# First norm's statistics from a second, row-wise copy of the input, loaded in four parts, with the inverse roots broadcast through a line in HBM

## The chip, the cores and the metric

The kernel runs on one core of a Trainium2 chip. The metric is the device time of one execution in microseconds. The times of the kernel before are the median, the lowest and the highest of three runs; one execution more was taken by the hardware profiler, and all rows of the profile come from that one.

## The reference, cut to what matters

A trunk of two layers on one sequence of 256 tokens with 2048 features, all in float32. The change touches only the first norm and the first projection; what follows in the same layer shows who reads their results.

```python
def rmsnorm(x, g):
    x32 = x.astype(jnp.float32)
    y = x32 * lax.rsqrt(jnp.mean(jnp.square(x32), axis=-1, keepdims=True) + NORM_EPS)
    return (y * g.astype(jnp.float32)).astype(x.dtype)

def short_conv_mixer(u, w_in, conv_w, w_out):
    proj = u @ w_in                                  # 2048 -> 3 * 2048
    xin, gate_c, gate_b = jnp.split(proj, 3, axis=-1)
    v = gate_c * xin
    S = v.shape[1]
    vp = jnp.pad(v, ((0, 0), (CONV_WIDTH - 1, 0), (0, 0)))
    conv = sum(conv_w[k] * vp[:, k:k + S] for k in range(CONV_WIDTH))
    return (gate_b * conv) @ w_out

# layer 0
u = rmsnorm(h, mix_pre_g[0])
m = short_conv_mixer(u, a_w_in[0], a_conv_w[0], a_w_out[0])
h = h + rmsnorm(m, mix_post_g[0])
...                                                  # squared-ReLU MLP, shared K and V,
                                                     # layer 1: stick-breaking attention, MLP
```

## The kernel before

Every float32 product is made of three matmuls of rounded parts: each weight and each input is split into a high part (ACT rounds it, `whi`, L174 or L219) and a low part (DVE subtracts, `wlo`, L185). Weights come in chunks of 128x1024 (512 KB) on SP's queue, five raw buffers deep (`RAW`), and their parts live in a ring of seven (`RING`). `chunk` asks for the splits up to four chunks ahead of the one in use (`AHEAD`).

The order of the instructions on PE is that of the program text. On DVE, ACT and POOL a planner of the framework fixes an order when the program is built, from priorities that follow the text and from its own estimate of when operands are there; on the chip each engine then runs its list strictly in order. A piece of work that the text asks for late can therefore stand early in an engine's list.

The first stage is `convolution`. The input comes transposed (`xT`, features on the partitions, 256 tokens in a row). The norm's gain is multiplied in at once (`enter`), but the norm's factor, one number per token, only after the projection, since it scales whole columns: `r` is the inverse root for each token, on all partitions, and `r2` its square (for the product of two projections).

- In the lead, six tiles of the projection (`lead`) are computed side by side over the 16 input blocks. Meanwhile `squares` makes the squares of the input on ACT (L836) and adds them up on DVE (L838, L840).
- Then come the units of `IN_UNITS`: tiles 0 to 3, then sixteen times a pair and a tile (tiles 4 to 19), then tiles 20 to 25. A tile is 16 high and 16 low matmuls (L813) into one PSUM bank; `IN_BANKS` gives banks 0, 1 and 7 to tiles 0, 1, 2, and bank 6 to tiles 3 to 19. So from tile 4 on, a tile can't start before the bank has been emptied of the one before, by `combined`: ACT copies one half (`half`, L820), DVE adds the other (`sum`, L822). A pair is 21 matmuls of 512 columns (L922 to L924, seven block products in the manner of Strassen and Winograd) that needs sums of input blocks (`sums_of_pair`, L903 to L911) and of weight blocks (`split_seven`, L211). After the eighth pair seven additions on DVE (L933) collect the first result.
- `statistics` runs after tile 0: the two halves of `acc` are added, two passes of a matmul with a matrix of 1/2048 (`ms`, L851) sum over the partitions and spread the result over all of them, and then follow a root on ACT, a reciprocal of 128x256 and a square on DVE.
- `conv_tile` takes three finished tiles (input, gate C, gate B) through product, scaling by `r2`, convolution, scaling by `r` and splitting for the next projection. It is called after tiles 1, 2, 4, 5, 8, 11, 14 and 17; the first and the third of these take the tiles of the lead.
- After tile 21 the text asks for the rows of `x` that the residual needs (`h`, L982, on POOL's queue).

`x4` is a tag with eight buffers of 8 KB per partition: `u` takes four, the last `xsums` two, and `y4` follows.

Of the kernel before, what the change touches and what calls it, by code (L numbers as in the profile page):

```python
# [45 lines left out]
LATER = 7  # L46
# [50 lines left out]
def trunk(ctx, tc, x, xT, vecs, rows, ws, out):  # L97
# [8 lines left out]
    wsplit = ctx.enter_context(tc.tile_pool(name="ws", bufs=RING))  # L106
    psum = ctx.enter_context(tc.tile_pool(name="ps", bufs=1, space=bass.MemoryType.PSUM))
# [663 lines left out]
    def convolution(tmp):  # L771
# [27 lines left out]
        acc = tmp.tile([P, 2 * T], F32, tag="acc", name="acc", bufs=1)  # L799
# [17 lines left out]

        def combined(ps):
            b = tiny("half")
            nc.scalar.activation(b[:], ps[:, T:], AF.Copy)  # L820
            s = tiny("sum", bufs=LEAD + 2)
            nc.vector.tensor_tensor(s[:], ps[:, :T], b[:], op=ALU.add)  # L822
            return s
# [9 lines left out]
        def squares(q, behind):  # L833
            sq = tmp.tile([P, 2 * T], F32, tag="sq", name="sq", bufs=1)
            with tc.issue_after(entered[behind].ins):
                nc.scalar.activation(sq[:], hpair[q], AF.Square)  # L836
            if q == 0:
                nc.vector.tensor_copy(acc[:], sq[:])  # L838
            else:
                nc.vector.tensor_tensor(acc[:], acc[:], sq[:], op=ALU.add)  # L840

# [3 lines left out]
        mean = tmp.tile([P, P], F32, name="mean")  # L845
        nc.vector.memset(mean[:], 1.0 / D)

        def statistics():
            nc.vector.tensor_tensor(acc[:, :T], acc[:, :T], acc[:, T:], op=ALU.add)
            ps = bank(LEAD - 1, "ms")  # L850
            nc.tensor.matmul(ps[:, :T], mean[:], acc[:, :T], start=True, stop=True)  # L851
            r, r2 = tiny("rstd", bufs=1), tiny("rstd2", bufs=1)
            nc.scalar.activation(r[:], ps[:, :T], AF.Sqrt, bias=eps[:])
            nc.vector.reciprocal(r[:], r[:])
            nc.vector.tensor_tensor(r2[:], r[:], r[:], op=ALU.mult)
            scale["r"], scale["r2"] = r, r2

# [94 lines left out]
        for kind, i in IN_UNITS:  # L952
# [10 lines left out]
            if not scale:  # L963
                statistics()
            s = combined(ps)
            if n >= 2 * KD + KD // 2:
                gates[n - 2 * KD] = s
            else:
                new.append(s)
                if lead and len(new) == 2:  # L970
                    conv_tile(LEAD // 3 - len(lead) // 3, *lead[:3])
                    del lead[:3]
                if len(new) == 3:
                    conv_tile(n - 2 * KD, *new)
                    new = []
            if i == KD + 3:
# [571 lines left out]
```

## Time and profile before

| | |
|---|---|
| median of three runs | 2097.27 us (2096.62 to 2098.21) |
| the profiled execution | 2096.79 us, of it 2095.0 us span |
| granted TensorE clock of that execution | 0.998 |
| busy: PE, PE weight load, DVE, ACT, POOL | 99%, 85%, 90%, 70%, 5% of the span |
| lead of the first stage | to about 42 us |
| pairs and tiles of the first stage | about 42 to 260 us |

Times of rows count from the start of the span, in microseconds. A row of the timeline has the start, the duration, the engine, the line, the operation, output and inputs, the shape, how many were merged, and in brackets how long the engine was idle before and what ended that. A row of a group has the busy time and the mean duration in nanoseconds. A row of the waits has the total, the number and the longest. A row of DMA issues has the size of one and the median time from its issue to its landing.

### The profile page before, as it was taken

The page shows a single profiled execution, that of the slowest core. Times are in us where ns is not written, and L with a number is a line of the kernel's source. Part 1 is how long each engine was busy: PE and PEld are TensorE (multiplying, and loading weights), DVE is VectorE, ACT ScalarE, POOL GpSimd, SP SyncE. Part 2 cuts the span into 40 slices and gives each one's busy share as a digit, 9 for nine tenths or more (in the row PEclk, how much of TensorE's full clock was granted, in tenths as well). Part 3 has the DMA queues.
Part 4 walks back from the last instruction along what each step waited for, and adds up shares of the span by engine and source line. Part 5 has one row for each costly group of instructions (what it writes and reads, how often), then busy time and mean ns, then how long its engine had stood idle before and what let it go on. Part 6 is the DMA issues. An engine that isn't in the chain of part 4 may idle for free.

```text
span 2095.0 us, 29733 instructions
## 1 busy us (share of the span) xinstructions
PE 2079.7 (99%) x10566; PEld 1774.8 (85%) x10566; DVE 1888.3 (90%) x2811; ACT 1456.1 (70%) x2132; POOL 112.6 (5%) x137
## 2 busy tenths in 40 slices
PE   9999999999999999999999999999999999999998
PEld 8888888888888888888888888889888888888886
DVE  8999996999999999999766777658999999999997
ACT  8666554776777777777567888547877767677773
POOL 0000000000100101001000000000001010010010
PEclk9999999999999999999999999999999999999999
DMA  8467674677778878779575555665687787787884
GB/s 291 149 204 251 199 248 155 193 231 227 239 221 234 237 217 251 224 230 261 181 220 167 161 161 161 221 181 171 181 256 232 221 241 225 233 245 219 232 241 164
DMA packets 132341, 449.23 MB, mean 214 GB/s; under 512 B 14816, under 2 KB 15072, under 8 KB 131168
## 3 DMA queue, kind: packets, MB, share of 16 engines
q1 hardware_dynamic: 113184, 406.55, 60.9%
q0 software_dynamic: 18720, 40.38, 9.7%
q8 instruction: 83, 1.36, 0.3%
q14 instruction: 66, 0.54, 0.1%
q10 hardware_dynamic: 288, 0.39, 0.1%
HBM read 413.19 MB, written 2.10 MB: 198 GB/s over the span
## 4 chain that ended last, share of the span: by engine, by line
PE 94%; DVE 4%; issue 1%; DMA 1%; ACT 0%; SPq 0%; DVEq 0%; ACTq 0%
PE up L1081 21%; PE up L1088 12%; PE acc L327 7%; PE acc L329 7%; PE acc L328 7%; PE more L1195 5%; PE more L1194 5%; PE more L1196 5%; PE acc L813 5%; PE acc L1194 4%; PE acc L1195 4%; PE acc L1196 4%; DVE wlo L185 1%; PE up L1083 1%; PE tr L264 1%
## 5 line engine op out<-in xcount | busy, mean ns | idle before, releaser
L185 DVE TENSOR_TENSOR wlo<-raw,whi 128x1024 fp32r<-128x1024 f32 (+1 forms) x414 | 495.9, 1207 | 67.6 <-ACT whi L174 67.3
L174 ACT ACTIVATE whi<-raw 128x1024 fp32r<-128x1024 f32 (+1 forms) x414 | 424.7, 1044 | 152.3 <-PE acc L329 63.5
L1081 PE MATMUL up<-u,whi 128*128 128x512 f32 x1952 | 465.0, 389 | 0.0
L1081 PEld LDWEIGHTS up<-u,whi 128*128 128x128 f32 x1952 | 365.0, 188 | 74.7
L1088 PEld LDWEIGHTS up<-u,wlo 128*128 128x128 f32 x2048 | 263.6, 191 | 10.3
L1088 PE MATMUL up<-u,wlo 128*128 128x256 f32 x2048 | 268.1, 283 | 0.0
L211 DVE TENSOR_TENSOR sums<-raw,sums 128x512 f32<-128x512 f32 x260 | 179.3, 690 | 0.9
L187 DVE SCALAR_TENSOR_TENSOR wlo<-raw,gv,whi 128x512 fp32r<-128x512 f32 (+1 forms) x160 | 131.9, 854 | 41.7 <-ACT whi L174 40.9
L174 ACT ACTIVATE whi<-raw,gv 128x512 fp32r<-128x512 f32 (+1 forms) x160 | 121.6, 800 | 48.6 <-PE acc L329 42.2
L327 PE MATMUL acc<-whi,u 128*128 128x512 f32 x384 | 153.1, 399 | 0.1
L329 PE MATMUL acc<-whi,u 128*128 128x512 f32 x384 | 149.9, 390 | 0.0
L328 PE MATMUL acc<-wlo,u 128*128 128x512 f32 x384 | 149.8, 390 | 0.0
L1094 ACT ACTIVATE half<-up 128x256 f32<-128x256 f32 x128 | 49.1, 385 | 129.8 <-PE up L1088 127.2
L1101 POOL DMA_DIRECT2D mg<-more x108 | 94.0, 870 | 825.8 <-ACT more L1156 423.9
L813 PE MATMUL acc<-u,whi 128*128 128x512 f32 x416 | 98.9, 391 | 2.7 <-DVE sum L822 2.7
L211 DVE TENSOR_TENSOR sums<-raw,raw 128x512 f32<-128x512 f32 x130 | 89.8, 691 | 7.2 <-DMA raw<-w_mlp 7.1
L813 PEld LDWEIGHTS acc<-u,whi 128*128 128x128 f32 x416 | 77.4, 188 | 20.5 <-DVE sum L822 3.7
L211 DVE TENSOR_TENSOR sums<-raw 128x512 f32<-128x512 f32 x130 | 89.8, 691 | 2.2 <-DMA raw<-w_mlp 1.6
L329 PEld LDWEIGHTS acc<-whi,u 128*128 128x128 f32 x384 | 72.1, 188 | 15.4
L327 PEld LDWEIGHTS acc<-whi,u 128*128 128x128 f32 x384 | 72.2, 188 | 13.9 <-ACT tk L1380 0.6
L328 PEld LDWEIGHTS acc<-wlo,u 128*128 128x128 f32 x384 | 72.3, 188 | 13.4
L1034 ACT ACTIVATE s<-s 128x256 f32<-128x256 f32 x128 | 52.1, 411 | 12.1 <-DVE s L1033 11.6
(6686 smaller groups left out, 4589.3 us busy)
## 6 DMA issues: line engine op xcount, KB each, us to landing
raw<-w_mlp SPq DMA_DIRECT2D x512, 512.0 KB, 4.6
raw<-w_in SPq DMA_DIRECT2D x94, 512.0 KB, 4.5
mg<-more POOLq DMA_DIRECT2D x108, 256.0 KB, 6.2
raw<-w_out SPq DMA_DIRECT2D x32, 512.0 KB, 4.6
raw<-w_v SPq DMA_DIRECT2D x32, 512.0 KB, 4.5
raw<-w_k SPq DMA_DIRECT2D x32, 512.0 KB, 4.4
raw<-w_q SPq DMA_DIRECT2D x32, 512.0 KB, 4.3
raw<-w_wo SPq DMA_DIRECT2D x32, 512.0 KB, 3.8
```

The source lines that it names most:

```text
L174: rounded = nc.scalar.activation(hi[:, at], raw[i][:, at], AF.Copy, scale=1.0 if gain is None else gain)
L185: nc.vector.tensor_tensor(lo[:, at], t[:, at], hi[:, at].bitcast(F32), op=ALU.subtract)
L211: nc.vector.tensor_tensor(t, x, y, op=ALU.subtract)
L327: nc.tensor.matmul(ps[:], xh, hi[:, a], start=i == 0 and k == 0, stop=False)
L328: nc.tensor.matmul(ps[:], xh, lo[:, a], start=False, stop=False)
L329: nc.tensor.matmul(ps[:], xl, hi[:, a], start=False, stop=i == self.n - 1 and k == self.ks - 1)
L813: nc.tensor.matmul(ps[:, :cols], w, xs[:, :cols], start=k == 0 and part == parts[0], stop=k == KD - 1 and part == parts[1], skip_group_che ...
L1081: nc.tensor.matmul(ps, weight(0, first, m), x, start=k == 0, stop=False)
L1088: nc.tensor.matmul(pss[n][:, :T], weight(1, first, m), x, start=False, stop=k == KD - 1)
L1194: nc.tensor.matmul(self.ps[key][:], xh, hi, start=first, stop=False)
L1195: nc.tensor.matmul(self.ps[key][:], xh, lo, start=False, stop=False)
L1196: self.done = nc.tensor.matmul(self.ps[key][:], xl, hi, start=False, stop=last)
```

## The change

The squares of the transposed input, their sums and the matmul with `mean` are gone. Instead the input is loaded a second time in its own layout, tokens on the partitions, into two tiles of the tag `x4`, in four parts of 128x1024, on POOL's queue. Each load waits until ACT has copied the half of a certain tile: part 0 behind tile 0, parts 1 and 2 behind tile 1, part 3 behind tile 2. ACT squares the parts in place, each with its sum over the row, behind the half of tile 2 (parts 0, 1) and tile 3 (parts 2, 3). After tile 3, `statistics` adds the two sums of each block of 128 tokens, takes the inverse root there (one number per partition), and stores it into a line of 256 numbers in HBM; one further transfer reads that line to all 128 partitions. `r2` is a square on ACT, asked for after tile 5. The convolutions wait in a list: from tile 5 on, one is taken from it after each tile, so that they come after tiles 5, 6, 7, 8, 9, 11, 14 and 17. The tag `sum` has four buffers more.

```diff
-LATER = 7
+ROWS_AT = {0: (0,), 1: (1, 2), 2: (3,)}
+SQUARES_AT = {2: (0, 1), 3: (2, 3)}
+STATISTICS_AT = 3
...
+    scratch = ctx.enter_context(tc.tile_pool(name="line", bufs=1, space=bass.MemoryType.DRAM))
...
+        copied = {}
+
         def combined(ps):
             b = tiny("half")
-            nc.scalar.activation(b[:], ps[:, T:], AF.Copy)
-            s = tiny("sum", bufs=LEAD + 2)
+            copied["last"] = nc.scalar.activation(b[:], ps[:, T:], AF.Copy)
+            s = tiny("sum", bufs=LEAD + 6)
             nc.vector.tensor_tensor(s[:], ps[:, :T], b[:], op=ALU.add)
             return s
...
-        def squares(q, behind):
-            sq = tmp.tile([P, 2 * T], F32, tag="sq", name="sq", bufs=1)
-            with tc.issue_after(entered[behind].ins):
-                nc.scalar.activation(sq[:], hpair[q], AF.Square)
-            if q == 0:
-                nc.vector.tensor_copy(acc[:], sq[:])
-            else:
-                nc.vector.tensor_tensor(acc[:], acc[:], sq[:], op=ALU.add)
...
+        def load_piece(q, behind):
+            b, c = q // 2, q % 2
+            if c == 0:
+                xrows.append(act.tile([P, D], F32, tag="x4", name="xrows"))
+            load = nc.gpsimd.dma_start(
+                xrows[b][:, c * D // 2 : (c + 1) * D // 2], x[b * P : (b + 1) * P, c * D // 2 : (c + 1) * D // 2]
+            )
+            tc.add_manual_dep(
+                load.ins, behind.ins.name,
+                mybir.DependencyInfo(mybir.DependencyClass.Sync, mybir.DependencyReason.DATA), reason="later",
+            )
+
+        def square_piece(q, behind):
+            b, c = q // 2, q % 2
+            if c == 0:
+                sq.append(small("ss", 4))
+            a = xrows[b][:, c * D // 2 : (c + 1) * D // 2]
+            with tc.issue_after(behind.ins):
+                nc.scalar.activation(a, a, AF.Square, accum_out=sq[b][:, c : c + 1])
 
         def statistics():
-            nc.vector.tensor_tensor(acc[:, :T], acc[:, :T], acc[:, T:], op=ALU.add)
-            ps = bank(LEAD - 1, "ms")
-            nc.tensor.matmul(ps[:, :T], mean[:], acc[:, :T], start=True, stop=True)
+            line = scratch.tile([1, T], F32, name="line")
+            with tc.high_priority():
+                for b in range(NB):
+                    nc.vector.tensor_tensor(sq[b][:, 0:1], sq[b][:, 0:1], sq[b][:, 1:2], op=ALU.add)
+                    r = inverse_root(sq[b][:, 0:1], eps[:])
+                    nc.gpsimd.dma_start(line[:, b * P : (b + 1) * P].rearrange("o t -> t o"), r[:])
             r, r2 = tiny("rstd", bufs=1), tiny("rstd2", bufs=1)
-            nc.scalar.activation(r[:], ps[:, :T], AF.Sqrt, bias=eps[:])
-            nc.vector.reciprocal(r[:], r[:])
-            nc.vector.tensor_tensor(r2[:], r[:], r[:], op=ALU.mult)
+            nc.gpsimd.dma_start(r[:], line[:].to_broadcast([P, T]))
             scale["r"], scale["r2"] = r, r2
+
+        def squared():
+            nc.scalar.activation(scale["r2"][:], scale["r"][:], AF.Square)
...
-            if k % 2 and LATER <= k + 2 < KD:
-                squares((k + 2 - LATER) // 2, k + 2)
-        for q in range((KD + 1 - LATER) // 2, KD // 2):
-            squares(q, KD - 1)
         lead = [combined(ps) for ps in pss]
+        waiting = [(i, *lead[3 * i : 3 * i + 3]) for i in range(LEAD // 3)]
...
-            if not scale:
+            s = combined(ps)
+            for q in ROWS_AT.get(i, ()):
+                load_piece(q, copied["last"])
+            for q in SQUARES_AT.get(i, ()):
+                square_piece(q, copied["last"])
+            if i == STATISTICS_AT:
                 statistics()
-            s = combined(ps)
+            if i == STATISTICS_AT + 2:
+                squared()
             if n >= 2 * KD + KD // 2:
                 gates[n - 2 * KD] = s
             else:
                 new.append(s)
-                if lead and len(new) == 2:
-                    conv_tile(LEAD // 3 - len(lead) // 3, *lead[:3])
-                    del lead[:3]
                 if len(new) == 3:
-                    conv_tile(n - 2 * KD, *new)
+                    waiting.append((n - 2 * KD, *new))
                     new = []
+                if waiting and i >= STATISTICS_AT + 2:
+                    conv_tile(*waiting.pop(0))
```

The existing helper that `statistics` now calls:

```python
def inverse_root(total, bias, scale=1.0 / D):
    r = small("rstd")
    nc.scalar.activation(r[:], total, AF.Sqrt, bias=bias, scale=scale)
    nc.vector.reciprocal(r[:], r[:])
    return r
```

More of the change, by code (lines that the diff above doesn't have):

```diff
@@ L798, in convolution @@
         u = [operand("u4") for _ in range(4)]
-        acc = tmp.tile([P, 2 * T], F32, tag="acc", name="acc", bufs=1)
         warm = bank(7, "warm")
@@ L831, in convolution @@
         entered = {}
-        def squares(q, behind):
-            sq = tmp.tile([P, 2 * T], F32, tag="sq", name="sq", bufs=1)
-            with tc.issue_after(entered[behind].ins):
-                nc.scalar.activation(sq[:], hpair[q], AF.Square)
-            if q == 0:
-                nc.vector.tensor_copy(acc[:], sq[:])
-            else:
-                nc.vector.tensor_tensor(acc[:], acc[:], sq[:], op=ALU.add)
         y = [None] * 4
         scale = {}
-        mean = tmp.tile([P, P], F32, name="mean")
@@ L846, in convolution @@
-        nc.vector.memset(mean[:], 1.0 / D)
-        def statistics():
-            nc.vector.tensor_tensor(acc[:, :T], acc[:, :T], acc[:, T:], op=ALU.add)
-            ps = bank(LEAD - 1, "ms")
-            nc.tensor.matmul(ps[:, :T], mean[:], acc[:, :T], start=True, stop=True)
+        xrows, sq = [], []
+        def load_piece(q, behind):
[9 more added lines that the diff above has]
+            )
```

## The prediction

> **What bounds the kernel now.** I read the page first, then the busy times by stage, then the waits of PE in the stage that the diff touches, then the starts of PE's and DVE's instructions there.
>
> ```profile
> span 2095.0 us, 29733 instructions
> PE 2079.7 (99%) x10566; PEld 1774.8 (85%) x10566; DVE 1888.3 (90%) x2811; ACT 1456.1 (70%) x2132; POOL 112.6 (5%) x137
> 15.00:42.00 27.00, 26.89 (x155) 23.42 (x153) 26.97 (x42) 23.26 (x37) 0.00 (x0) 1.00 0.91 297
> 42.00:66.00 24.00, 23.44 (x133) 20.71 (x134) 23.66 (x53) 17.73 (x33) 0.00 (x0) 1.00 0.46 155
> 66.00:120.00 54.00, 52.12 (x265) 43.73 (x265) 54.00 (x83) 32.85 (x44) 0.00 (x0) 1.00 0.61 191
> 120.00:180.00 60.00, 59.16 (x297) 49.89 (x296) 59.96 (x87) 35.16 (x44) 0.69 (x1) 1.00 0.64 215
> PE acc L813 <- DVE sum L822: 3.4, 5, 0.8
> ```
>
> The columns of the stage rows are PE, PEld, DVE, ACT, POOL, granted clock, DMA share, GB/s. PE is full nearly everywhere; the whole kernel has 15.3 us of idle PE (2095.0 less 2079.7). The diff touches only the first stage. There DVE has next to no idle time from 15 to 180 us, and PE has 3.28 us of it between 42 and 180 (0.56, 1.88 and 0.84). One kind of wait makes 3.4 us, in five places: a tile of the first projection may not start before DVE has run the `sum` (L822) that empties its PSUM bank of the tile before. DVE runs behind, so the sum comes late.
>
> The starts of the tiles on PE (and of two pairs, `more`) give the loss:
>
> ```profile
> 42.56 2.17 PE L813 MATMUL acc<-u,wlo 128*128 128x256 f32 x16 [0.67 <-DVE sum L822]
> 48.22 0.59 PE L851 MATMUL ms<-acc,mean 128*128 128x256 f32 x2
> 48.47 4.02 PE L813 MATMUL acc<-u,whi 128*128 128x512 f32 x16
> 65.35 0.40 PE L922 MATMUL more<-whi20a,u 128*128 128x512 f32 x1
> 71.01 3.88 PE L813 MATMUL acc<-u,whi 128*128 128x512 f32 x16 [0.72 <-DVE sum L822]
> 76.64 0.40 PE L922 MATMUL more<-whi24a,u 128*128 128x512 f32 x1
> 81.43 3.79 PE L813 MATMUL acc<-u,whi 128*128 128x512 f32 x16
> 92.24 3.93 PE L813 MATMUL acc<-u,whi 128*128 128x512 f32 x16 [0.33 <-DVE sum L822]
> 103.75 3.92 PE L813 MATMUL acc<-u,whi 128*128 128x512 f32 x16 [0.84 <-DVE sum L822]
> 114.20 3.79 PE L813 MATMUL acc<-u,whi 128*128 128x512 f32 x16
> 145.18 3.79 PE L813 MATMUL acc<-u,whi 128*128 128x512 f32 x16
> 167.14 3.92 PE L813 MATMUL acc<-u,whi 128*128 128x512 f32 x16 [0.83 <-DVE sum L822]
> ```
>
> Tiles 8 to 11 start at 114.20 and, three periods on, 145.18: a pair and a tile without a wait take 10.33 us. Against that tile 4 is 0.87 late (the pair at 65.35 needs 4.79, as the one from 76.64 to 81.43 does), tile 5 0.09 (10.42 from 71.01), tile 6 0.48, tile 7 1.18, tile 8 0.12, and tiles 12 and 13 together 1.30 (21.96 for two periods): 4.0 us. With 0.67 at tile 0 and 0.25 for the `ms` matmuls (48.22 to 48.47) the stage has 5.0 us to give, 0.24% of the kernel. That is the ceiling.
>
> What sets DVE's pace is seen in four of its sums, those of tiles 4 to 7:
>
> ```profile
> 80.27 0.42 DVE L822 TENSOR_TENSOR sum<-acc,half 128x256 f32<-128x256 f32 x1
> 91.77 0.42 DVE L822 TENSOR_TENSOR sum<-acc,half 128x256 f32<-128x256 f32 x1
> 103.27 0.42 DVE L822 TENSOR_TENSOR sum<-acc,half 128x256 f32<-128x256 f32 x1
> 112.28 0.43 DVE L822 TENSOR_TENSOR sum<-acc,half 128x256 f32<-128x256 f32 x1
> ```
>
> From sum to sum DVE takes 11.50 us with a `conv_tile` between (after tiles 4 and 5) and 9.01 without. Against PE's 10.33, a period without it gives DVE back 1.32 us, one with it costs 1.17.
>
> **What is removed.** On DVE:
>
> ```profile
> L840 DVE TENSOR_TENSOR acc<-acc,sq 128x512 f32<-128x512 f32 x7 | 4.8, 682 | 0.0
> L854 DVE RECIPROCAL rstd<-rstd 128x256 f32<-128x256 f32 x1 | 1.8, 1753 | 0.0
> ```
>
> With three short ones of the size of a sum (L838, L849, L855, about 0.42 each) that is 7.8 us, some 7 without the overlap of neighbours. About 5 of it lies before 42 us, where PE does not wait; the sums for the pairs (`sums_of_pair`) can move into that hole, so it counts later. PE loses the `ms` matmuls, and ACT eight squares in the lead, hidden there.
>
> **What is added.** The four pieces of x, 512 KB each, are issued from about 49 to 61 us (behind the `half` of tiles 0, 1, 1, 2). POOL's queue holds nothing else until the load of `h` below; SP's queue is not touched.
>
> ```profile
> 49.00:68.00 19.00, 19.00 (x108) 16.65 (x107) 19.00 (x41) 14.27 (x26) 0.00 (x0) 1.00 0.31 87
> 165.95 0.69 POOL L982 DMA_DIRECT2D h<-x  x1 [164.52 <-PE more L924]
> h<-x POOLq DMA_DIRECT2D x2, 1024.0 KB, 6.4
> out<-h SPq DMA_DIRECT2D x6, 256.0 KB, 2.1
> L174 ACT ACTIVATE whi<-raw 128x1024 fp32r<-128x1024 f32 (+1 forms) x414 | 424.7, 1044 | 152.3 <-PE acc L329 63.5
> L452 DVE RECIPROCAL rstd<-rstd 128x1 f32<-128x1 f32 x14 | 2.0, 158 | 6.6 <-ACT rstd L451 6.6
> L451 ACT ACTIVATE rstd<-hs,eps 128x1 f32<-128x1 f32 x6 | 1.5, 285 | 1.8 <-DVE hs L615 1.8
> 65.55 0.38 ACT L820 ACTIVATE half<-acc 128x256 f32<-128x256 f32 x1 [0.22 <-PE acc L813]
> 77.64 0.36 ACT L820 ACTIVATE half<-acc 128x256 f32<-128x256 f32 x1
> ```
>
> 2 MB over these 19 us are 110 GB/s; with the 87 there, 197, where 297 flowed from 15 to 42: the weights lose nothing. ACT gets four squares of 128x1024 (1.04 each, as the rounding of that size) and a small one for r2, where it is busy 32.85 of 54 us: hidden, unless they wait. DVE gets four instructions of about 0.16: 0.6 us.
>
> **When the roots arrive.** The last piece is issued at about 61 and lands by 67.4 (at 6.4 a load); the squares stand behind the `half` at 65.55, so the last ends near 68.6, and sum, root and reciprocal take 0.6 (0.16, 0.29, 0.16): 69.3. Then two transfers follow one another, the store of the line and the broadcast. No row shows a store of four bytes per partition. Bounds: 2.1 us each (the output stores) and 6.4 each (`h`): r at 73.5 or at 82. I take 3 each, nearer the store, since little data moves: 75 to 76. The first `conv_tile` is due after tile 5, which ends near 86, so even the late end is in time, if nobody asks sooner.
>
> The Trainium skill, "DMA: Bandwidth & Descriptors", section "Anatomy of one DMA — SWDGE (gpsimd) path", gives a transfer from this queue about 2.0 us plus its bytes at 436 GB/s; for the megabyte of `h` that is an estimated 4.4 us, and the trace's 6.4 is longer. With that rule r would arrive near 73.5, and the sum below would stay.
>
> **What moves.** This term decides. `conv_tile` ran after tiles 1, 2, 4, 5, 8, 11; now after 5, 6, 7, 8, 9, 11. Before tile 5 DVE is freer by some 12 us (7 removed, two convolutions of 2.49, 11.50 less 9.01, put off) but cannot bank all that: the weight buffers fill, and a sum cannot run before its tile ends. How far ahead it can be is seen where it has caught up, at tile 17 and the start of tile 18; the additions of L933 matter below:
>
> ```profile
> 214.73 0.42 DVE L822 TENSOR_TENSOR sum<-acc,half 128x256 f32<-128x256 f32 x1
> 218.90 3.79 PE L813 MATMUL acc<-u,whi 128*128 128x512 f32 x16
> L933 DVE TENSOR_TENSOR mg<-mg,more 128x512 f32<-128x512 f32 x4 | 2.7, 684 | 0.0
> L933 DVE TENSOR_TENSOR mg<-mg,acc 128x512 f32<-128x512 f32 x3 | 2.0, 684 | 0.0
> ```
>
> The sum ends at 215.15: 3.75 us of slack at most. Five convolutions in a row cost 1.17 each: slack 2.58, 1.41, 0.24, then waits of 0.93 and 1.17. Right behind come the seven additions of the first result, 4.7 busy, some 4.2 on the path (before, they met 2.8 us of slack saved up from tile 7 on: 1.32, 1.32, less 1.17, 1.32): 9.01 + 4.2 - 10.33 = 2.9 of wait; the convolution after tile 11 makes another 1.17. Sum 6.2. If half of the first convolution slips into DVE's gap before tile 5's sum (1.32), it is 4.9. With 0.12 of restart behind each wait (as at tile 8), and 0.3 to 0.67 left at tile 0, where removed instructions stood ahead of the first sums, the loss is 5.6 to 7.3 against 5.0: between +0.6 and +2.3. I take +1.2, nearer the low end, because the gaps do exist. The profiled execution took 2096.79 us, so 2098.0; the median of the three runs is 0.48 above it, so 2098.5.
>
> **Rivals.** *Slower: ACT is caught waiting for r.* The order of ACT and DVE is fixed when the program is built. r2 may be placed where the builder thinks that r has come, ahead of tile 4's `half` (77.64 now, near 77.0 when ACT is free). At 3 us a transfer that costs nothing; at 6.4 ACT stands until 82, that `half` is some 5.4 us late, and so is its sum. The slack of 3.75 is gone with 1.7 of wait; one free tile returns 1.32, then five convolutions (5.85), the additions (2.9) and the next convolution (1.17) come as waits: 10.3, with about 1 of restarts and 0.3 at tile 0 11.6, some 6.6 more than before: 2103.9. It decides when r2 stands ahead of that `half` and r comes after about 81. Against it: the program asks for r2 only after tile 5. For it: the builder does move work far ahead; this belongs to the pair sums asked for at tile 0:
>
> ```profile
> 4.14 0.49 ACT L903 ACTIVATE xa<-gx 128x256 f32<-128x256 f32 x1
> ```
>
> A wait of DVE at `v` (L866) has the same price. The Trainium skill, "SBUF — State Buffer", section "Who interferes with whom", speaks against the route: descriptors of transfers from the GpSimd queue cannot be written while VectorE copies in its two-port modes. In this trace the `h` load, issued while DVE is busy 59.96 of 60 us, occupied POOL for 0.69 us, no sign of it; DVE's work there has two inputs.
>
> *Faster: DVE's freed time is really used.* r comes at 73.5 and the gaps hold the three waiting convolutions by tile 7. Then slack is 3.75 until the next one: 2.58, 1.41, then waits of 1.5 and 1.17, with restarts and tile 0 about 3.2 us, 1.8 less than before: 2095.5, still no difference. Only if the additions also find room do nearly all 5.0 go: 2092.3 to 2093. Against it: the slack is never above 3.75.
>
> *The change does nothing for DVE's deadline*: the removed work leaves holes only where PE did not wait, and just `ms` goes: 2097.0.
>
> **How the numbers follow.** A measurement of this kernel can tell about 0.2%, 4.2 us: below 2093.1 is faster, above 2101.5 slower. The forecast (0.38), its small gain (0.08) and `ms` alone (0.06), all inside, make 0.52; the wait on r or on another late transfer gets 0.33; the full gain 0.15. The range holds the forecast, the edge of the gain, and the wait with 1.8 us for bounds not met: 2093.0 to 2105.7.
>
> **What would show it.** Right: DVE with gaps between 42 and 75, no PE wait at tiles 4 and 6, waits on `sum` bunched at tiles 10 to 13, five convolutions between 86 and 140, no L851. Wrong: r landing after 81 with a long wait of ACT at r2 or of DVE at `v` (slower); no wait on `sum` from tile 9 on (faster); ACT waiting over 2 us for a piece of x.

## Result, and the profile after

The changed kernel took 2109.52 us in the median (2108.85 to 2111.14, four runs), the kernel before 2097.67 on the same chip: ratio 1.0057 [1.0045, 1.0068]. The change makes the kernel slower by 0.57%, where 2098.5 us and at most 2105.7 were forecast. The profiled execution has a span of 2107.8 us against 2095.0: 12.8 us to explain.

First the page's span and the busy times by stage of the changed kernel (columns PE, PEld, DVE, ACT, POOL, granted clock, DMA share, GB/s):

```profile
span 2107.8 us, 29731 instructions
15.00:42.00 27.00, 26.66 (x156) 23.21 (x155) 25.78 (x46) 22.65 (x39) 0.00 (x0) 1.00 0.93 321
42.00:66.00 24.00, 24.00 (x133) 20.93 (x132) 21.72 (x40) 16.44 (x30) 2.83 (x5) 1.00 0.84 215
66.00:120.00 54.00, 47.74 (x229) 39.11 (x228) 41.48 (x65) 28.16 (x39) 1.08 (x2) 0.94 0.69 169
120.00:180.00 60.00, 53.47 (x259) 44.58 (x258) 59.73 (x93) 33.28 (x44) 0.10 (x1) 0.94 0.56 179
```

DVE now has the idle time that was meant to come: 2.3 us between 42 and 66 us, where PE is full. Then PE itself loses 6.26 us from 66 to 120 and 6.53 from 120 to 180. In the first of these stretches DVE is idle for 12.5 us as well, and the DMA moves only 169 GB/s: somebody else is late. In the second DVE is full. So there are two different losses, and the starts of the tiles on PE say where each lies:

```profile
40.55 2.18 PE L815 MATMUL acc<-u,wlo 128*128 128x256 f32 x16 [0.34 <-DVE sum L826]
77.99 3.79 PE L815 MATMUL acc<-u,whi 128*128 128x512 f32 x16
85.94 0.50 PE L938 MATMUL more<-wlo28a,u 128*128 128x512 f32 x1 [2.02 <-DVE wlo28a L188]
89.78 0.80 PE L937 MATMUL acc<-whi28b,u 128*128 128x512 f32 x1 [3.11 <-ACT whi28b L222]
96.98 3.92 PE L815 MATMUL acc<-u,whi 128*128 128x512 f32 x16 [0.38 <-DVE sum L826]
107.44 3.79 PE L815 MATMUL acc<-u,whi 128*128 128x512 f32 x16
118.22 3.94 PE L815 MATMUL acc<-u,whi 128*128 128x512 f32 x16 [0.29 <-DVE sum L826]
129.45 3.96 PE L815 MATMUL acc<-u,whi 128*128 128x512 f32 x16 [0.59 <-DVE sum L826]
140.95 3.96 PE L815 MATMUL acc<-u,whi 128*128 128x512 f32 x16 [0.84 <-DVE sum L826]
156.72 6.54 PE L815 MATMUL acc<-u,whi 128*128 128x512 f32 x16 [5.11 <-DVE sum L826]
```

| start of tile | before | after | difference |
|---|---|---|---|
| 0 | 42.56 | 40.55 | -2.0 |
| 5 | 81.43 | 77.99 | -3.4 |
| 6 | 92.24 | 96.98 | +4.7 |
| 10 | 134.86 | 140.95 | +6.1 |
| 11 | 145.18 | 156.72 | +11.5 |
| 12 | 155.64 | 169.79 | +14.2 |

Up to tile 5 the change is ahead by 3.4 us. Between tiles 5 and 6 it loses 8.2. From tile 6 to 10 it loses 1.4, at tile 11 5.4, behind that 2.6 more. Before, tiles 12 and 13 lost 1.3 that are not lost now, which leaves the 12.8. Against 10.33 us behind tile 5, tile 6 is 8.7 late. PE's waits there add up to 6.0 (2.02, 3.11, 0.46 and 0.38), and behind them TensorE is slow: its granted clock is 0.50 from 89 to 92 us.

The loss before tile 6 is seen on ACT, with the `half` of tile 4 and what follows it, and on DVE:

```profile
76.41 0.37 ACT L824 ACTIVATE half<-acc 128x256 f32<-128x256 f32 x1
88.36 0.42 ACT L874 ACTIVATE rstd<-rstd 128x256 f32<-128x256 f32 x1 [11.58 <-DMA rstd<-line]
88.69 1.04 ACT L222 ACTIVATE whi28b<-raw 128x1024 fp32r<-128x1024 f32 x1
```

```profile
83.99 0.69 DVE L214 TENSOR_TENSOR sums<-raw,raw 128x512 f32<-128x512 f32 x1 [6.14 <-DMA raw<-w_in]
```

L874 is r2. It was placed right behind tile 4's `half`, though the text asks for it after tile 5, and ACT stood there for 11.58 us until r came; PE's pair waits for `whi28b` behind it. But DVE waited too, 6.14 us, and not for r: for a block of weights. PE's wait of 2.02 us, for `wlo28a`, hangs on this one, its wait of 3.11, for `whi28b`, on ACT's. Why both were late is in the issues on POOL's queue (first line: start of the issue; idle before it) and in the times from issue to landing, of the whole run for the line and of the loads issued from 58 to 80 us for `raw`:

```profile
69.55 0.54 POOL L868 DMA_DIRECT2D line<-rstd  x1 [6.68 <-DVE rstd L455]
84.34 0.54 POOL L870 DMA_DIRECT2D rstd<-line  x1 [14.25 <-DMA line<-rstd]
```

```profile
line<-rstd POOLq DMA_DIRECT2D x2, 0.5 KB, 11.1
rstd<-line POOLq DMA_DIRECT2D x1, 128.0 KB, 4.0
raw<-w_in SPq DMA_DIRECT2D x6, 512.0 KB, 11.8
```

The same answer of the kernel before, and then the changed kernel's stages while the two stores are under way:

```profile
raw<-w_in SPq DMA_DIRECT2D x7, 512.0 KB, 3.7
```

```profile
62.40:66.00 3.60, 3.60 (x20) 3.07 (x19) 3.60 (x6) 3.60 (x9) 0.47 (x1) 1.00 1.24 23
66.00:69.60 3.60, 3.60 (x18) 2.98 (x17) 2.93 (x9) 3.60 (x7) 0.05 (x1) 1.00 0.68 35
72.00:75.00 3.00, 3.00 (x20) 2.70 (x19) 1.25 (x2) 0.41 (x1) 0.00 (x0) 1.00 0.70 274
```

Two stores of 512 bytes each take 8.0 and 14.3 us (11.1 is their middle). The broadcast, 256 times as much, takes 4.0. From 62.4 to 69.6 us, with the first store under way, the DMA engines are as busy as otherwise (shares of 1.24 and 0.68) but move 23 and 35 GB/s. Traffic comes back while the second is still to land (274 GB/s from 72 to 75 us). The weight loads issued from 58 to 80 us land after 11.8 us instead of 3.7. That is a fact of one profile; whether the store is the cause, and which of the two waits costs the time, was for the runs to say.

### The profile page after: what moved, and what is told of

Its sections match the earlier page's. It is cut to its first block, busy times and chain, and to the rows that moved or that the text cites. A ratio compares the mean times of both kernels' runs of the same rounds, so it can differ in the third digit from the quotient of the medians.

```text
span 2107.8 us, 29731 instructions
## 1 busy us (share of the span) xinstructions
PE 2084.2 (99%) x10564; PEld 1776.6 (84%) x10564; DVE 1884.8 (89%) x2803; ACT 1455.9 (69%) x2134; POOL 116.4 (6%) x144
## 4 chain that ended last, share of the span: by engine, by line
PE 94%; DVE 3%; DMA 1%; issue 1%; ACT 1%; SPq 0%; DVEq 0%; ACTq 0%; POOLq 0%
PE up L1101 21%; PE up L1108 12%; PE acc L330 7%; PE acc L332 7%; PE acc L331 7%; PE more L1215 5%; PE more L1214 5%; PE more L1216 5%; PE acc L815 5%; PE acc L1214 4%; PE acc L1215 4%; PE acc L1216 4%; PE lead L815 1%; PE up L1103 1%; PE tr L267 1%
## 5 line engine op out<-in xcount | busy, mean ns | idle before, releaser
L190 DVE SCALAR_TENSOR_TENSOR wlo<-raw,gv,whi 128x512 fp32r<-128x512 f32 (+1 forms) x160 | 131.9, 854 | 41.6 <-ACT whi L177 40.8
L1054 ACT ACTIVATE s<-s 128x256 f32<-128x256 f32 x128 | 52.0, 410 | 10.9 <-DVE s L1053 10.2
```

## The experiments

My theory after the result had three parts: the store of four bytes per partition is slow and starves the weight loads; r2 holds ACT; and the bunched convolutions cost more behind tile 10 than I had forecast. The main rival was that one part explains it all.

**The store made wide.** The line becomes 256 rows of 128 copies. The broadcast reads 256 numbers in one stretch that touches both stores, so this kernel leaves out that every token gets its own root; the rest stays. (Three dots in a diff stand for lines left out.)

```diff
-            line = scratch.tile([1, T], F32, name="line")
+            line = scratch.tile([T, P], F32, name="line")
...
-                    nc.gpsimd.dma_start(line[:, b * P : (b + 1) * P].rearrange("o t -> t o"), r[:])
+                    wide = tiny("wide", bufs=2, cols=P)
+                    nc.vector.tensor_scalar(wide[:], ones[:], r[:], None, op0=ALU.mult)
+                    nc.gpsimd.dma_start(line[b * P : (b + 1) * P, :], wide[:])
...
-            nc.gpsimd.dma_start(r[:], line[:].to_broadcast([P, T]))
+            nc.gpsimd.dma_start(r[:], line[P - 1 : P + 1, :].rearrange("a b -> (a b)").unsqueeze(0).to_broadcast([P, T]))
```

> The changed kernel, but each inverse root is copied along its partition and stored as a row of 128 numbers (512 bytes per partition, 64 KB per store), and the broadcast reads one whole stretch of 256 numbers that touches both stores. It leaves out that every token gets its own root. Theory 'small writes': the store of 4 bytes per partition is what is slow and what holds the DMA engines, so here each store lands within 4 us, r comes by about 76, no weight load takes over 8 us, ACT does not stand at r2, and tile 6 starts near 88.3 in place of 96.98: about 8.5 us less than the changed kernel, 2101. The bunch of convolutions stays: waits on the sum from tile 9 to tile 11. Rival 'the way through HBM': a store followed by a dependent load is slow whatever its rows; then ACT still stands 10 us and the time is 2108 to 2110.

Measured: 2098.78 us, ratio 1.0005 [0.9996, 1.0014], span 2096.7, some 2 us below the 2101 expected. The landings (the second line for loads issued from 58 to 80 us), a stage, and the starts of tiles 6 and 11:

```profile
line<-wide POOLq DMA_DIRECT2D x2, 64.0 KB, 2.8
raw<-w_in SPq DMA_DIRECT2D x8, 512.0 KB, 4.3
66.00:72.00 6.00, 6.00 (x30) 5.03 (x29) 5.41 (x13) 6.00 (x11) 0.54 (x1) 1.00 0.86 280
88.63 3.79 PE L815 MATMUL acc<-u,whi 128*128 128x512 f32 x16
146.86 5.36 PE L815 MATMUL acc<-u,whi 128*128 128x512 f32 x16 [5.11 <-DVE sum L826]
```

With 128 times the bytes the store takes a quarter of the time, the weights land nearly as before, 280 GB/s flow from 66 to 72 us where the changed kernel moves 34, and no wait is left at tile 6. This one store, with all that hangs on it, is worth 11.1 of the 12.8 us of span. What remains is the change as I had forecast it, nearly at the time that I had forecast; how far for the right reasons, is told below.

**The hold.** r2 stands behind the `half` of tile 6, and the convolutions begin one tile later (with one more buffer for `sum`); the small stores stay.

```diff
-            nc.scalar.activation(scale["r2"][:], scale["r"][:], AF.Square)
+            with tc.issue_after(copied["last"].ins):
+                nc.scalar.activation(scale["r2"][:], scale["r"][:], AF.Square)
...
-            if i == STATISTICS_AT + 2:
+            if i == STATISTICS_AT + 3:
...
-                if waiting and i >= STATISTICS_AT + 2:
+                if waiting and i >= STATISTICS_AT + 3:
```

> The changed kernel, with r2 placed behind the half of tile 6 in ACT's list and the convolutions from tile 6 on. Theory 'the hold': ACT standing 11.6 us at r2 is the whole of the 8.7 us that PE loses before tile 6; here that goes, time about 2101. Rival 'starved weights': while the small stores are under way the weights land after 11 to 18 us, so DVE still waits for the raw weights of the third pair until about 84 and tile 6 is still 3 to 6 us late: 2104 to 2107.

Measured: 2102.08 us, 1.0019 [1.0009, 1.0029], span 2100.8, between the two expectations. The weight loads still land after 10.5 us. Tile 6 is late as the rival has it:

```profile
92.82 3.94 PE L815 MATMUL acc<-u,whi 128*128 128x512 f32 x16 [1.91 <-DVE sum L826]
```

That is 3.5 us later than 10.33 behind tile 5 (at 79.01), where the changed kernel is 8.7 late. So the hold is a part, and not the whole. Of the 7.0 us of span that this run gains, 5.2 lie between tiles 5 and 6 and 3.7 between tiles 6 and 12, where the convolutions moved too; 1.0 is lost at tile 0 and 0.7 at tile 13.

**The starving.** wide_store, with two more stores of the old kind that nobody reads.

```diff
+            thin = scratch.tile([1, T], F32, name="thin")
...
+            for b in range(NB):
+                nc.gpsimd.dma_start(thin[:, b * P : (b + 1) * P].rearrange("o t -> t o"), ones_of[b][:])
```

> wide_store with two more stores that nobody reads, 4 bytes per partition each, issued on the GpSimd queue behind the broadcast (about 76 us), when weight loads are in flight (278 GB/s from 75 to 80 in wide_store). Theory 'starved weights': the weight loads issued beside them land after 10 us or more in place of 4.4, DVE and ACT run dry, and PE loses 2 to 5 us: 2101 to 2104. Rival 'only the waiting counts': as wide_store, 2098 to 2099.5.

Measured: 2107.34 us, 1.0045 [1.003, 1.006], 8.6 us above wide_store and above the range of both theories. The unread stores did not come behind the broadcast, at about 76 us: they were issued at 62.80 and 69.91, each ahead of its wide store. The unread stores, the weight loads issued from 58 to 80 us, and ACT's waits in that region:

```profile
thin<-rstd POOLq DMA_DIRECT2D x2, 0.5 KB, 10.9
raw<-w_in SPq DMA_DIRECT2D x6, 512.0 KB, 11.0
```

```profile
83.61 1.06 ACT L222 ACTIVATE whi28b<-raw 128x1024 fp32r<-128x1024 f32 x1 [6.74 <-DMA raw<-w_in]
88.04 0.42 ACT L881 ACTIVATE rstd<-rstd 128x256 f32<-128x256 f32 x1 [3.37 <-DMA rstd<-line]
```

Here `whi28b` stands ahead of r2 and waits 6.74 us for its own weights. The wide stores come behind the small ones and r is late again, so a hold of 3.37 us is left; tile 6 is 6.6 us late. Two small stores in flight are enough to bring most of the loss back, whether their data are needed or not. How the 8.6 us divide between the starved weights and the late r, this run does not separate.

**Another queue.** The changed kernel with its small stores issued by ACT.

```diff
-                    nc.gpsimd.dma_start(line[:, b * P : (b + 1) * P].rearrange("o t -> t o"), r[:])
+                    nc.scalar.dma_start(line[:, b * P : (b + 1) * P].rearrange("o t -> t o"), r[:])
```

> The changed kernel with the two small stores (4 bytes per partition) issued on ACT's queue in place of the GpSimd queue, all else the same. Theory 'small writes': what is slow is the 128 writes of 4 bytes, whatever queue they come from; each store still takes 7 us or more to land and the weight loads beside it over 10 us: 2106 to 2111. Rival 'the GpSimd queue': from ACT's queue a store lands in about 2.3 us as the outputs do, and the time is that of wide_store, 2098 to 2100.

Measured: 2108.12 us, 1.0049 [1.0034, 1.0064]; stores landing after 10.1 us in the median, weight loads after 10.6, ACT's hold 10.50. Which queue issues the stores makes no difference that these runs can tell.

**The small stores in the kernel before**, about 52 us in, with nobody to read them.

```diff
+            line = scratch.tile([1, T], F32, name="line")
+            for b in range(NB):
+                nc.gpsimd.dma_start(line[:, b * P : (b + 1) * P].rearrange("o t -> t o"), r[:, b : b + 1])
```

> The kernel before plus only the two stores of 4 bytes per partition into a line in HBM, issued on the GpSimd queue when the roots are known (about 51 us); nothing reads the line. Theory 'starved weights': each store needs 8 to 14 us to land, the weight loads issued beside them land after 10 us or more in place of 4.5, and since DVE has no slack at that point PE loses 2 to 9 us: 2099 to 2106. Rival 'only the waiting counts': nothing waits for the line, so 2097 to 2098.

Measured: 2097.06 us, 0.9999 [0.9989, 1.0008]. They land after 6.9 us, but between 54 and 58 us nothing else is being loaded:

```profile
line<-rstd POOLq DMA_DIRECT2D x2, 0.5 KB, 6.9
```

```profile
54.00:58.00 4.00, 4.00 (x29) 3.70 (x28) 4.00 (x12) 2.43 (x6) 0.00 (x0) 1.00 0.00 0
```

The DMA engines' busy share is 0.00 in these 4 us, though both stores are still to land: their 6.9 us are not time in which the engines are seen at work. So the price of such a store is not its own time but what is in flight beside it. In this empty stretch it cost nothing that can be told.

**How wide is wide enough?** wide_store with 16 and with 64 copies, rows of 64 and 256 bytes (the width of `line`, of the part of `wide` that is stored, and the rows that the broadcast reads).

```diff
-            line = scratch.tile([T, P], F32, name="line")
+            line = scratch.tile([T, 16], F32, name="line")
...
-                    nc.gpsimd.dma_start(line[b * P : (b + 1) * P, :], wide[:])
+                    nc.gpsimd.dma_start(line[b * P : (b + 1) * P, :], wide[:, :16])
```

> wide_store with 16 copies of a root for each token instead of 128: rows of 64 bytes, 128 of them in a store as before; the broadcast reads 16 such rows (not every token's own root). Theory A (what is dear is an element of a few bytes; it grows as elements shrink, and 64 bytes are 16 times as many as 4): stores land in 3 to 4 us, weight loads issued from 58 to 80 us in about 5, time 2099 to 2101. Theory B (every element below that of wide_store, 512 bytes, is written in the same slow way, 256 times in a row): stores land in 8 to 14 us, weight loads in about 10, time 2105 to 2110. The Trainium skill, "DMA: Bandwidth & Descriptors", section "Specifications", has transfers below 512 bytes read, changed and written back, which is B if that is what costs.

> wide_store with 64 copies: rows of 256 bytes, the broadcast reads 4 of them (not every token's own root). Theory A (small elements are dear by their smallness): as wide_store, stores landing in about 2.8 us, time 2098 to 2100. Theory B (all below 512 bytes are alike): stores land in 8 to 14 us, time 2105 to 2110. With copies_16 slow and this one fast the bound lies between 64 and 256 bytes.

Measured: 2098.82 us, 1.0008 [0.9999, 1.0017], and 2099.0 us, 1.0005 [0.9996, 1.0014]. Both land their stores after 2.9 us and their weights after 4.4. Theory A holds in both, and rows of 64 bytes are as good as rows of 512. The rule of the Trainium skill that the expectation cites covers both, since both have rows below 512 bytes, and neither was slow.

**Four bytes, set apart.** That left two readings: elements of four bytes are slow, or elements that lie side by side. wide_small again, with the unread four bytes of each token 64 bytes from the next.

```diff
-            thin = scratch.tile([1, T], F32, name="thin")
+            thin = scratch.tile([T, 16], F32, name="thin")
...
-                nc.gpsimd.dma_start(thin[:, b * P : (b + 1) * P].rearrange("o t -> t o"), ones_of[b][:])
+                nc.gpsimd.dma_start(thin[b * P : (b + 1) * P, :1], ones_of[b][:])
```

> wide_small (wide_store with two more stores of four bytes per partition, which nobody reads), but the four bytes of each token now lie 64 bytes from those of the next instead of behind them. Theory A (an element of four bytes is slow in itself): landing about 11 us, weight loads issued from 58 to 80 us landing in about 11, time 2105 to 2109 as wide_small. Theory B (elements that lie side by side in one short stretch of HBM hold each other up): with 64 bytes between them the stores land in some 3 us as the 64-byte rows of copies_16 do, the weight loads in 4 to 5, time 2098 to 2101.

Measured: 2099.18 us, 1.0007 [0.9997, 1.0017]; the two lines of wide_small again:

```profile
thin<-rstd POOLq DMA_DIRECT2D x2, 0.5 KB, 3.3
raw<-w_in SPq DMA_DIRECT2D x8, 512.0 KB, 4.5
```

The same 256 elements of four bytes, in as many bytes and as many packets (19472 on POOL's queue over the whole run, in both), land in 3.3 us instead of 10.9 and hold up nothing that the run shows. The two runs differ only in where the elements lie: next to each other, 256 separate writes into one KB of HBM, or 64 bytes apart. Whether they hold each other up because they share a short stretch, or whether most are slow because they do not start at a multiple of 64 bytes, wasn't tried, and neither was a distance below 64 bytes. Which unit of the memory is behind it stays open.

**The bunch alone.** The kernel before, with its statistics where they were, and the convolutions put off to tiles 5, 6, 7, 8, 9 and 11 as in the change.

```diff
+        waiting = [(i, *lead[3 * i : 3 * i + 3]) for i in range(LEAD // 3)]
...
-                if lead and len(new) == 2:
-                    conv_tile(LEAD // 3 - len(lead) // 3, *lead[:3])
-                    del lead[:3]
                 if len(new) == 3:
-                    conv_tile(n - 2 * KD, *new)
+                    waiting.append((n - 2 * KD, *new))
                     new = []
+                if waiting and i >= 5:
+                    conv_tile(*waiting.pop(0))
```

> The kernel before with one part of the change: the convolutions are put off to tiles 5, 6, 7, 8, 9, 11, its own statistics stay. Theory 'the bunch': five convolutions in a row and then the seven additions leave no slack; in the changed kernel tiles 7 to 13 lose 8.2 us more than before, here the same waits come, with a wait over 4 us before tile 11 and a slow clock behind it, against some 1.5 us saved at tiles 4 to 7: 2101 to 2105. Rival 'the bunch is harmless': the planner spreads them, 2096 to 2098.5.

Measured: 2099.94 us, 1.0007 [0.9998, 1.0017], span 1.9 above the kernel before. That lies between the two expectations, and the interval holds 1, so the time alone decides nothing. Its two waits of PE from tile 0 on:

```profile
42.41 2.17 PE L813 MATMUL acc<-u,wlo 128*128 128x256 f32 x16 [1.95 <-DVE sum L822]
147.07 5.27 PE L813 MATMUL acc<-u,whi 128*128 128x512 f32 x16 [4.64 <-DVE sum L822]
```

All small waits from tile 4 on are gone, and one of 4.64 us stands in their place, as in wide_store (5.11). The rows of DVE point to the order of its list. Here are the first and the last of the seven additions and tile 10's sum in wide_store, then the same sum and the first addition in the kernel before:

```profile
140.97 0.68 DVE L950 TENSOR_TENSOR mg<-mg,more 128x512 f32<-128x512 f32 x1
145.10 1.28 DVE L950 TENSOR_TENSOR mg<-mg,acc 128x512 f32<-128x512 f32 x2
146.29 0.42 DVE L826 TENSOR_TENSOR sum<-acc,half 128x256 f32<-128x256 f32 x1
```

```profile
141.82 0.42 DVE L822 TENSOR_TENSOR sum<-acc,half 128x256 f32<-128x256 f32 x1
144.09 0.69 DVE L933 TENSOR_TENSOR mg<-mg,more 128x512 f32<-128x512 f32 x1
```

The additions have a high priority. With five convolutions before them, the planner put them ahead of the sum that PE needs first. What this order costs, the next run shows.

**The order alone.** wide_store, with that sum given the same priority.

```diff
-            s = combined(ps)
+            with tc.high_priority() if i == 10 else contextlib.nullcontext():
+                s = combined(ps)
```

> wide_store with tile 10's half and sum given the priority that the seven additions of the first result have, so that this sum stands ahead of them in VectorE's list, as it does in the kernel before; nothing else is changed. Theory (the 5.1 us wait at tile 11 and the low clock behind it come from that order): the wait goes, tile 11 starts near 141.7 instead of 146.9 with its high part at 3.8 us instead of 5.4, and what is left are waits of some 1 to 3 us in later periods, since VectorE still has the same work to do: span 2091 to 2093, median 2094 to 2096. Rival (VectorE's work in these periods is the bound, whatever its order): the additions come 5 us later instead, the pair behind them or a later tile waits as long for its banks, and the time stays at 2098 to 2099.

Measured: 2096.6 us, 0.9996 [0.9987, 1.0005], span 2094.7, so 2.0 below wide_store, where 4 to 6 were expected and the rival expected none. Tile 11 starts at 141.18, 5.7 us earlier than in wide_store and without a wait, but then:

```profile
PE more L940 <- DVE wlo52a L188: 1.7, 1, 1.7
PE acc L940 <- DVE wlo52b L188: 0.8, 1, 0.8
```

The next pair now waits for its weights, split by the same DVE, and TensorE is slow again behind these waits: its granted clock is 0.75 from 148 to 152 us and 0.83 from 152 to 156. Tile 12 starts at 155.86, only 2.9 us earlier than in wide_store. Both theories were half right: the order costs some 2 us, and the rest stays, as waits on DVE in these periods that this order does not take away.

**The bunch dissolved.** wide_store with the convolutions (`CONV_AT`) after tiles 5, 6, 8, 12, 14, 16, 17 and 18.

```diff
-                if waiting and i >= STATISTICS_AT + 2:
-                    conv_tile(*waiting.pop(0))
+            if i in CONV_AT:
+                conv_tile(*waiting.pop(0))
```

> wide_store (wide rows to HBM, not every token's own root) with the convolutions spread out: after tiles 5, 6, 8, 12, 14, 16, 17, 18 in place of 5, 6, 7, 8, 9, 11, 14, 17. Theory 'the bunch': wide_store is no faster than before only because the convolutions in a row push the sum of tile 10 behind the seven additions, which makes PE wait 5.1 us and then run at a low clock; here that sum stands ahead of them, tile 11 starts near 140.3 in place of 146.9, and the time is 2090 to 2093, 0.3% below before. Rival 'DVE has no room anyway': the additions and the late convolutions bring the same waits a few tiles later, 2097 to 2099.

Measured: 2096.21 us, 0.9993 [0.9983, 1.0002], span 1.6 below wide_store. PE has no wait from tile 4 to tile 18 and one of 1.13 us at tile 19, and the next projection starts at 266.02, where wide_store starts it at 271.66 and the kernel before at 269.85. Just behind, most of the gain is given back:

```profile
270.44 0.50 PE L331 MATMUL acc<-whi,y 128*128 128x512 f32 x1 [2.19 <-DVE sum L827]
```

```profile
272.00:276.00 4.00, 4.00 (x12) 3.14 (x11) 4.00 (x7) 1.24 (x2) 0.00 (x0) 0.58 0.97 352
```

The work put off ends DVE's stage later: its last sum comes 2.19 us late, and then TensorE runs at a granted clock of 0.58 for these 4 us, by estimate another 1.7 us (0.42 of 4). So the time is nearer to the rival's range than to the theory's.

**No line at all.** The roots go to all partitions through TensorE: a diagonal matrix of them (`ident` times r, on DVE) is multiplied by ones behind tile 3. The pieces are loaded one step earlier, the convolutions come after tiles 4, 5, 7, 12, 14, 16, 17 and 18.

```diff
-                    nc.gpsimd.dma_start(line[:, b * P : (b + 1) * P].rearrange("o t -> t o"), r[:])
+                    dg = tiny("diag", bufs=2, cols=P)
+                    nc.vector.tensor_scalar(dg[:], ident[:], r[:], None, op0=ALU.mult)
+                    diagonals.append(dg)
...
+            ps = bank(LEAD - 1, "ms")
+            for b, dg in enumerate(diagonals):
+                nc.tensor.matmul(ps[:, b * P : (b + 1) * P], ones[:], dg[:], start=True, stop=True)
...
-            nc.gpsimd.dma_start(r[:], line[:].to_broadcast([P, T]))
+            with tc.high_priority():
+                nc.scalar.activation(r[:], ps[:, :T], AF.Copy)
+                nc.scalar.activation(r2[:], ps[:, :T], AF.Square)
```

> The same statistics from the second copy, but without the line in HBM: the inverse roots of 128 tokens scale an identity matrix on DVE (128x128, twice), and two small matmuls with a matrix of ones behind tile 3 put them on all partitions in a PSUM bank; ACT copies r and r2 from there. The parts of x are issued one step earlier (behind the lead, tile 0 twice, tile 1), the convolutions come after tiles 4, 5, 7, 12, 14, 16, 17, 18. If small writes, hold and bunch are the whole of the loss, PE waits for no sum until tile 12, r is there by 65 us, and the time is 2089 to 2093, 0.2 to 0.4% below before. Rival: the extra squares and loads in the lead cost as much as the freed DVE brings, 2096 to 2099.

Measured: 2094.18 us, 0.9984 [0.9975, 0.9994], span 2091.4, a little above the 2093 expected. How much of the 2.0 us below wide_spread is due to the missing line and how much to the other tiles of the convolutions, was not separated. One wait of size is left: the second diagonal stands late in DVE's list.

```profile
65.47 0.49 PE L876 MATMUL ms<-diag,ones 128*128 128x128 f32 x2 [2.16 <-DVE diag L869]
```

So the last run loads and squares the pieces one tile earlier:

```diff
-ROWS_AT = {0: (1, 2), 1: (3,)}
-SQUARES_AT = {1: (0,), 2: (1, 2, 3)}
+ROWS_AT = {0: (2,), 1: (3,)}
+SQUARES_AT = {1: (0, 1), 2: (2, 3)}
...
+        load_piece(1, copied["last"])
```

> pe_spread (roots put on all partitions by TensorE, eight conv_tiles spread out) with the pieces and squares one tile earlier: all four squares lie behind the half of tiles 1 and 2, and the second diagonal stands in VectorE's list ahead of the two weight remainders that made it late. Theory (TensorE's 2.2 us wait for the diagonal was all that pe_spread still lost in this stage, and nothing comes in its place): the ms matmuls follow tile 3 without a wait, span some 2.2 us below pe_spread's 2091.4, so 2089.2, median about 2092.0, ratio 0.9974. Rival (two pieces loaded at once behind the lead take bandwidth from the weights, or VectorE is late elsewhere by the same amount): a wait for raw or for a sum of 1 to 3 us appears, and the time stays at 2094.

Measured: 2091.59 us, 0.9974 [0.9965, 0.9983], span 2089.3: the theory, to 0.4 us. It beats the kernel before by 0.26%, and PE's busy time fills the stages:

```profile
62.85 0.60 PE L876 MATMUL ms<-diag,ones 128*128 128x128 f32 x4
```

```profile
66.00:120.00 54.00, 54.00 (x277) 46.24 (x277) 53.94 (x77) 35.38 (x44) 0.00 (x0) 1.00 0.67 212
120.00:180.00 60.00, 60.00 (x311) 51.56 (x310) 59.49 (x84) 37.28 (x45) 0.53 (x1) 1.00 0.69 224
```

## Why the prediction was wrong

*When the roots arrive: the step that failed.* The last square, the sum, root and reciprocal were right: the second store is issued at 69.55, where 69.3 was forecast for the root. The broadcast's 4.0 us lies within its bounds of 2.1 and 6.4. The store's 14.3 does not. Both bounds were taken from transfers of large rows, and the value "nearer the store, since little data moves": by bytes. The prediction said that no row shows such a store, and yet closed the term at 6.4. r came at about 88.3, 13 us after the forecast and 6 after the late end, with the long wait of ACT at r2 that was named as a sign of being wrong.

*"The weights lose nothing": the second failure, of the same kind.* The bandwidth was added up in bytes. For the 2 MB of x that held: loads of weights issued from 40 to 58 us land after 5.6 us instead of 4.5, with no wait. For the two stores of half a KB it didn't. No term of the sum stood for it. In wide_small it costs 8.6 us with data that nobody needs, a hold of 3.37 us included.

*The rival "ACT is caught waiting for r"* named the mechanism, the instruction and the planner's part, and was priced at 2103.9. It missed by 5.6 us: r came at 88.3 and not at 82, and the price had no starving. r2 stood behind tile 4's `half`, not ahead of it, so tile 5 was still on time and the pair behind it was late.

*What moves.* The convolutions in a row cost somewhat less than was forecast: waits of 0.93 and 1.17 us were to come at tiles 9 and 10, or 1.32 less if half of the first convolution slips into a gap. In wide_store DVE's lead lasts until tile 9, and tile 10 is 1.15 us late. Mis-sized was the step "right behind come the seven additions": 2.9 us of wait, and 1.17 at the next tile. Both came at once, at tile 11, since the additions stood ahead of the sum and not behind it: 5.1 us where 4.1 were forecast for both. The restart was taken as 0.12 for each wait. That is right for the short ones (the high part takes 3.92 to 3.96 us instead of 3.79) and wrong for the long one: 5.36 in wide_store, 1.6 more, and 6.54 in the changed kernel, 2.7 more.

*What is removed.* "About 5 of it lies before 42 us, where PE does not wait" was wrong in the other direction. Before, DVE is full in the lead (26.97 of 27 us), and what it is late there comes out at tile 0. Tile 0 starts at 42.56, 42.67 and 42.41 in the three kernels that keep the statistics in the lead (the kernel before, store_only and bunch_only), and between 40.4 and 41.6 in all others: some 1 to 2 us, of which the forecast counted at most 0.4. In wide_store this gain and the larger loss behind tile 10 nearly cancel. That its 2098.78 comes so near the forecast's 2098.5 is in part luck, and no proof of the forecast's working. The ceiling of 5.0 us, which had only 0.67 for tile 0, was too low for the same reason: pe_early gains 5.7 us of span.

*Sign and size.* The chance of slower was 0.33; the case that came nearest was in the list, at too low a price and without the starved weights. Had the store's time been left open upwards, as a transfer that no row resembles, the range would have reached past 2105.7.

## What to carry to other kernels

Don't write a column as many single elements next to one another in HBM: in this kernel two stores of 128 floats so written took 8.0 and 14.3 us and held up the weight loads beside them. A row of 64 bytes for each float, or a matmul with a diagonal in place of the line, took that away. A bound taken from rows must come from rows of the same shape; if there is none, leave the term open upwards, and ask what else uses the resource meanwhile. Work that is put off to free one deadline has to be placed again by the deadlines it lands on, and the order that the planner makes there must be read, not assumed.

## What the hardware showed that I had not expected

**Small neighbouring writes.** Two stores of 0.5 KB took 8.0 and 14.3 us to landing. From 66 to 72 us all transfers together moved 34 GB/s (280 in wide_store), and weight loads landed after 11.8 us instead of 3.7. With nothing beside them two such stores still took 6.9 us, and with 64 bytes between the elements 3.3 us, without harm. The Trainium skill, "DMA: Bandwidth & Descriptors", section "Specifications", has transfers of less than 512 bytes read, changed and written back. Rows of 256 and 64 bytes, and of four bytes set apart, showed no price here, so its border is not the one that mattered.

**The clock after a wait of PE.** Behind the wait of 5.11 us the changed kernel's TensorE runs with a granted clock of 0.55 from 156.7 to 163 us. The high part behind such a wait, 5.11 to 5.14 us long, took 5.36 us in wide_store, 6.00 in copies_64, 6.54 in the changed kernel, 6.61 in copies_16 and 6.71 in act_store (3.79 at full clock). For shorter waits there is no clear border: the clock dipped behind 2.19 us in wide_spread and behind 1.67 and 0.77 us in sum_first, and did not behind 2.16 us in pe_spread. Behind a single wait on a sum below 1 us the high part took 3.9 us. The Trainium skill, "TensorE: Matmul & The Clock Gate", section "What's actually happening", tells of a free-running window of about 3.4 us by which the clock is set. A price that varies with where the wait falls agrees with it. What decides for a wait of about 2 us, no run here shows.
